# Near-equal steps with a mixed sixth transfer, and a first load issued as two partition halves, in a relu-and-row-sum kernel

## Chip, cores and metric

The kernel runs on one core of a Trainium2 chip. The metric is the device time of one execution in microseconds (us). Profiles show a slightly shorter span than that time (162.8 us for a run timed at 164.56 us), because the span counts from the first to the last recorded work. Every run quoted here was fast, with a granted clock of 1.0.

Engine names in the profile: ACT is ScalarE, DVE is VectorE, SP is SyncE. SPq and ACTq are those engines' sequencers, which issue transfers (DMAs). A transfer has "landed" when its semaphore has received the last of its increments.

## The reference

```python
x = np.random.randn(32, 512, 1024).astype(np.float32)     # 64 MiB
relu_x = np.maximum(x, 0)
out = np.sum(relu_x, axis=-1).astype(np.float32)          # (32, 512)
```

There are 16,384 rows of 1,024 floats. Each of the 128 partitions handles 128 successive rows, so the input of a partition is one contiguous stretch of 512 KiB.

## The kernel before

The rows come in seven transfers of 16 rows per partition (8 MiB, 64 KiB contiguous per partition) into three buffers, then in a tail of 8, 4, 2, 1 rows and two half-rows. All loads are issued by SyncE. In the first six transfers ("two-pass"), ScalarE applies relu in place to a step of rows and VectorE sums that step; the steps are 2, 6 and 8 rows. In the seventh transfer and in the tail ("fused"), each engine takes alternate rows and does relu and sum in one instruction. Cuts are marked with `# ...`.

```python
BIG, NBIG, NTWO, NB = 16, 7, 6, 3
STEPS, TAIL, LAST = [2, 6, 8], [8, 4, 2, 1], [512, 512]
# ...
for c in range(NBIG + 1):
    if c >= NB:
        sp.wait_ge(s_dve, len(STEPS) * (c - NB + 1))       # buffer free
    if c < NBIG:
        sp.dma_start(
            out=buf[:, c % NB, :, :], in_=xv[:, c * BIG : (c + 1) * BIG, :]
        ).then_inc(s_in[c], 16)
# ... tail loads, same form
for c in range(NTWO):
    b, r = c % NB, 0
    act.wait_ge(s_in[c], 16)
    for i, n in enumerate(STEPS):
        t = buf[:, b, r : r + n, :]
        act.activation(t, t, AF.Relu).then_inc(s_act, 1)
        dve.wait_ge(s_act, len(STEPS) * c + i + 1)
        dve.tensor_reduce(out=res[:, c * BIG + r : c * BIG + r + n],
                          in_=t, axis=X, op=ALU.add).then_inc(s_dve, 1)
        r += n
# ... seventh transfer and tail: on_dve / on_act on alternate rows
# ... the two half-rows: both on VectorE, one after the other; then the store of res
```

Of the kernel before, what the change touches and what calls it, by code (L numbers as in the profile page):

```python
# [2 lines left out]

P = 128
D = 1024
BIG = 16
NBIG = 7
NTWO = 6
NB = 3
STEPS = [2, 6, 8]  # L10
TAIL = [8, 4, 2, 1]
LAST = [512, 512]


def bass_relu_sum_kernel(
    nc: bass.Bass,
    x: bass.AP,
    out: bass.AP,
):




    fp32 = mybir.dt.float32
    ALU = mybir.AluOpType
    AF = mybir.ActivationFunctionType
    X = mybir.AxisListType.X

    B, S, _ = x.shape
    J = B * S // P  # L30
    assert BIG * NBIG + sum(TAIL) + 1 == J and sum(LAST) == D

    xv = x.rearrange("b s d -> (b s) d").rearrange("(p j) d -> p j d", p=P)
    ov = out.rearrange("b s -> (b s)").rearrange("(p j) -> p j", p=P)

    buf = nc.alloc_sbuf_tensor("buf", [P, NB, BIG, D], fp32)
    last = nc.alloc_sbuf_tensor("last", [P, LAST[1] + 1], fp32)
    res = nc.alloc_sbuf_tensor("res", [P, J], fp32)

    n_in = NBIG + len(TAIL) + 2  # L40
    s_in = [nc.alloc_semaphore(f"s_in{i}") for i in range(n_in)]
    s_act = nc.alloc_semaphore("s_act")
    s_dve = nc.alloc_semaphore("s_dve")
    s_part = nc.alloc_semaphore("s_part")
    s_tact = nc.alloc_semaphore("s_tact")
    s_tdve = nc.alloc_semaphore("s_tdve")
    s_out = nc.alloc_semaphore("s_out")

    sp, act, dve = nc.sync, nc.scalar, nc.vector


    tb = NBIG % NB
    for c in range(NBIG + 1):
        if c >= NB:
            sp.wait_ge(s_dve, len(STEPS) * (c - NB + 1))
        if c < NBIG:
            sp.dma_start(  # L57
                out=buf[:, c % NB, :, :], in_=xv[:, c * BIG : (c + 1) * BIG, :]
            ).then_inc(s_in[c], 16)
    r = 0  # L60
    tail = []
    for i, n in enumerate(TAIL):
        sp.dma_start(
            out=buf[:, tb, r : r + n, :],
            in_=xv[:, NBIG * BIG + r : NBIG * BIG + r + n, :],
        ).then_inc(s_in[NBIG + i], 16)
        tail.append((r, n, s_in[NBIG + i]))
        r += n
    sp.dma_start(
        out=buf[:, tb, r, 0 : LAST[0]], in_=xv[:, J - 1, 0 : LAST[0]]  # L70
    ).then_inc(s_in[-2], 16)
    sp.dma_start(out=last[:, 0 : LAST[1]], in_=xv[:, J - 1, LAST[0] : D]).then_inc(
        s_in[-1], 16
    )


    for c in range(NTWO):
        b, r = c % NB, 0
        act.wait_ge(s_in[c], 16)
        for i, n in enumerate(STEPS):  # L80
            t = buf[:, b, r : r + n, :]
            act.activation(t, t, AF.Relu).then_inc(s_act, 1)  # L82
            dve.wait_ge(s_act, len(STEPS) * c + i + 1)
            dve.tensor_reduce(  # L84
                out=res[:, c * BIG + r : c * BIG + r + n], in_=t, axis=X, op=ALU.add
            ).then_inc(s_dve, 1)
            r += n


    def on_act(t, acc):  # L90
        return act.activation(t, t, AF.Relu, accum_out=acc)  # L91

    def on_dve(t, acc):
        return dve.tensor_scalar(  # L94
            out=t, in0=t, scalar1=0.0, scalar2=None, op0=ALU.max, op1=ALU.add, accum_out=acc
        )

    j0 = NBIG * BIG
    for c in range(NTWO, NBIG):
        act.wait_ge(s_in[c], 16)  # L100
        dve.wait_ge(s_in[c], 16)
        for i in range(BIG):
            f = on_act if i % 2 else on_dve
            f(buf[:, c % NB, i, :], res[:, c * BIG + i : c * BIG + i + 1])
    for r, n, s in tail:
        act.wait_ge(s, 16)
        if n > 1:
            dve.wait_ge(s, 16)
        for i in range(r, r + n):
            f = on_act if n == 1 or (i - r) % 2 else on_dve  # L110
            ins = f(buf[:, tb, i, :], res[:, j0 + i : j0 + i + 1])
            if f is on_act:
                last_act = ins
    last_act.then_inc(s_tact, 1)

    dve.wait_ge(s_in[-2], 16)
    on_dve(buf[:, tb, BIG - 1, 0 : LAST[0]], last[:, LAST[1] : LAST[1] + 1]).then_inc(s_part, 1)
    dve.wait_ge(s_part, 1)
    dve.wait_ge(s_in[-1], 16)
    on_dve(last[:, :], res[:, J - 1 : J]).then_inc(s_tdve, 1)  # L120


    sp.wait_ge(s_tact, 1)
    sp.wait_ge(s_tdve, 1)
    sp.dma_start(out=ov[:, :], in_=res[:, :]).then_inc(s_out, 16)
    sp.wait_ge(s_out, 16)


# [1 line left out]
_INS = ['x']  # L130
_OUTS = [((32, 512), 'float32')]


# [21 lines left out]
```

## Time and profile before

| What | Value | Where it is read |
|---|---|---|
| time | 164.67 us median (164.54 to 165.19, 3 runs) | run times |
| load queue busy | 96.1% of 16 DMA engines' span | queue table |
| steady period of an 8 MiB transfer | 19.35 us | starts of ACT in the timeline |
| first transfer landed | 23.1 us | first relu in the timeline |
| last load landed | 158.96 us | semaphore records |
| DVE done | 161.15 us | chain of waits |

From the page of the kernel before: the busy tenths of the DMA engines and the GB/s they moved, in 40 equal slices, and the row of the load queue (packets, MB, share of the time of 16 engines).

```profile
DMA  7979979979989998998997997997998997999980
GB/s 258 515 306 467 499 322 467 515 322 451 515 370 403 515 419 354 515 419 354 515 467 306 515 499 322 467 515 338 435 515 354 419 515 338 427 419 403 411 322 16
q1 hardware_dynamic: 2016, 67.18, 96.1%
```

The transfer engines are busy from the first slice to the last. The GB/s swing because a 64 KiB packet is counted in one slice; the mean over a longer stretch says more. This is such a stretch, from 5 to 20 us; the last two columns are the DMA share and GB/s.

```profile
core 0: us, DVE busy (x) ACT busy (x) POOL busy (x), PEclk, DMA share, GB/s
5.00:20.00 15.00, 0.00 (x0) 0.00 (x0) 0.00 (x0) 1.00 1.05 450
```

The timeline of ACT (start, length, instruction, and in brackets the idle time before it and what ended it):

```profile
0.72 1.28 ACT L82 ACT_TABLE_LOAD   x1 [0.72 <-PEq L140]
23.15 14.04 ACT L82 ACTIVATE buf<-buf 128x2048 f32<-128x2048 f32 x3 [21.14 <-DMA buf<-in_x_dram]
42.45 14.04 ACT L82 ACTIVATE buf<-buf 128x2048 f32<-128x2048 f32 x3 [5.26 <-DMA buf<-in_x_dram]
61.91 14.04 ACT L82 ACTIVATE buf<-buf 128x2048 f32<-128x2048 f32 x3 [5.42 <-DMA buf<-in_x_dram]
```

ACT needs 14 us of every 19.35 us and then waits for the next load. The end of the chain of waits (start, length, what):

```profile
134.03 8.69 DVE res L84
142.72 16.28 DVE buf L94 x29
159.00 0.73 issue
159.73 0.70 DVE buf L94 x3
160.43 0.02 issue
160.46 0.69 DVE last L94 x2
```

Here, at the end only, DVE is late. The eight-row reduce of the sixth transfer ends at 142.7 us, 3.4 us after the seventh has landed, and DVE works without a pause until 161.15 us, 2.2 us behind the last load. (The row of 0.73 us "issue" is not a pause of DVE: from 142.72 to 161.15 us it was busy for 18.39 of 18.43 us.)

### The profile page before, as it was taken

How to read it: one execution, taken by the hardware profiler on the slowest of the kernel's cores; microseconds unless marked ns; L12 is line 12 of the kernel's file. 1: busy time of each engine (PE TensorE's matmuls, PEld its weight loads, DVE VectorE, ACT ScalarE, POOL GpSimd, SP SyncE). 2: the span in 40 equal slices, each digit the busy share in tenths (PEclk: the TensorE clock that was granted, in tenths of full speed). 3: DMA queues.
4: the chain of work that ended last, by engine and by line, in shares of the span. 5: the costliest groups of instructions: out<-in, count | busy, mean ns of one | idle time of the engine just before them, and what ended most of it. 6: DMA issues, size and time to landing. Idle time of an engine off the chain costs nothing.

```text
span 162.8 us, 136 instructions
## 1 busy us (share of the span) xinstructions
DVE 123.1 (76%) x52; ACT 102.7 (63%) x51; POOL 0.2 (0%) x4
## 2 busy tenths in 40 slices
DVE  0000005599988999599996999969998799999995
ACT  3000039991599807996099942999159990796880
POOL 0000000000000000000000000000000000000000
DMA  7979979979989998998997997997998997999980
GB/s 258 515 306 467 499 322 467 515 322 451 515 370 403 515 419 354 515 419 354 515 467 306 515 499 322 467 515 338 435 515 354 419 515 338 427 419 403 411 322 16
DMA packets 2016, 67.18 MB, mean 413 GB/s; under 512 B 224, under 2 KB 352, under 8 KB 736
## 3 DMA queue, kind: packets, MB, share of 16 engines
q1 hardware_dynamic: 2016, 67.18, 96.1%
HBM read 67.11 MB, written 0.07 MB: 413 GB/s over the span
## 4 chain that ended last, share of the span: by engine, by line
DMA 47%; ACT 26%; DVE 22%; another core or an unknown queue 3%; issue 1%; SPq 0%
DMA buf<-in_x_dram 47%; ACT buf L82 26%; DVE res L84 11%; DVE buf L94 10%; DVE last L94 0%; SPq L57 0%
## 5 line engine op out<-in xcount | busy, mean ns | idle before, releaser
L84 DVE TENSOR_REDUCE res<-buf 128x2 f32<-128x2048 f32 (+2 forms) x18 | 104.7, 5839 | 38.0 <-ACT buf L82 38.0
L82 ACT ACTIVATE buf<-buf 128x2048 f32<-128x2048 f32 (+2 forms) x18 | 84.2, 4743 | 47.7 <-DMA buf<-in_x_dram 47.7
L91 ACT ACTIVATE buf<-buf 128x1024 f32<-128x1024 f32 x16 | 16.7, 1045 | 7.7 <-DMA buf<-in_x_dram 7.5
L94 DVE TENSOR_SCALAR_CACHE_REDUCE buf<-buf 128x1024 f32<-128x1024 f32 (+1 forms) x16 | 17.8, 1180 | 0.0
L91 ACT ACTIVATION_READ_ACCUMULATOR buf<-buf 128x1 f32 x16 | 3.0, 187 | 0.0
L82 ACT ACT_TABLE_LOAD x1 | 1.3, 1283 | 0.7 <-PEq L140 0.7
L94 DVE DVE_READ_ACCUMULATOR buf<-buf 128x1 f32 x16 | 1.3, 82 | 0.0
L94 DVE TENSOR_SCALAR_CACHE_REDUCE last<-last 128x513 f32<-128x513 f32 x1 | 0.7, 690 | 0.0
L140 POOL MEMSET const-bfloat16-1.0<- 128x1 bf16 x1 | 0.1, 102 | 0.0
L140 POOL MEMSET const-uint8-127<- 128x1 uint8 x1 | 0.1, 101 | 0.0
L140 POOL MEMSET const-float32-0.0<- 128x1 f32 x1 | 0.1, 99 | 0.2 <-issue 0.2
L140 POOL MEMSET const-float32-1.0<- 128x1 f32 x1 | 0.1, 98 | 0.0
L94 DVE DVE_READ_ACCUMULATOR last<-last 128x1 f32 x1 | 0.1, 82 | 0.0
## 6 DMA issues: line engine op xcount, KB each, us to landing
buf<-in_x_dram SPq DMA_DIRECT2D x1, 4096.0 KB, 25.6
buf<-in_x_dram SPq DMA_DIRECT2D x1, 2048.0 KB, 30.1
buf<-in_x_dram SPq DMA_DIRECT2D x1, 1024.0 KB, 32.1
buf<-in_x_dram SPq DMA_DIRECT2D x1, 512.0 KB, 32.9
buf<-in_x_dram SPq DMA_DIRECT2D x1, 256.0 KB, 33.1
last<-in_x_dram SPq DMA_DIRECT2D x1, 256.0 KB, 33.2
buf<-in_x_dram SPq DMA_DIRECT2D x7, 35.3
out_dram<-res SPq DMA_DIRECT2D x1, 64.0 KB, 1.5
```

The costliest lines, as they stand in the source:

```text
L82: act.activation(t, t, AF.Relu).then_inc(s_act, 1)
L84: dve.tensor_reduce(out=res[:, c * BIG + r : c * BIG + r + n], in_=t, axis=X, op=ALU.add).then_inc(s_dve, 1)
L91: return act.activation(t, t, AF.Relu, accum_out=acc)
L94: return dve.tensor_scalar(out=t, in0=t, scalar1=0.0, scalar2=None, op0=ALU.max, op1=ALU.add, accum_out=acc)
L140: nc = _bacc.Bacc("TRN2", target_bir_lowering=False, num_devices=1)
```

## The change

It has two independent parts. The first takes that VectorE backlog away: the two-pass steps become 4, 5, 7; in the sixth transfer four rows are done fused (two on each engine) and the other twelve in steps of 3, 4, 5; in the tail the single row goes to VectorE and the first half-row to ScalarE. `on_dve(*row(c, i))` and `on_act(*row(c, i))` are the fused instruction on row i of transfer c. The second part is meant to start the load stream sooner: the first transfer is cut into partitions 0 to 63 (from SyncE) and 64 to 127 (from ScalarE).

```diff
-STEPS = [2, 6, 8]
+STEPS = [4, 5, 7]
+MIXED = [3, 4, 5]
@@ loads
-        if c < NBIG:
+        if c == 0:
+            for q, h in ((sp, 0), (act, P // 2)):
+                q.dma_start(
+                    out=buf[h : h + P // 2, 0, :, :], in_=xv[h : h + P // 2, 0:BIG, :]
+                ).then_inc(s_in[0] if h == 0 else s_half, 16)
+        elif c < NBIG:
             sp.dma_start(out=buf[:, c % NB, :, :], ...)          # cut
@@ two-pass transfers
+        b, steps = c % NB, STEPS if c < NTWO - 1 else MIXED
         act.wait_ge(s_in[c], 16)
+        if c == 0:
+            act.wait_ge(s_half, 16)
+        if steps is MIXED:
+            dve.wait_ge(s_in[c], 16)
+            for i in (BIG - 4, BIG - 3):
+                on_dve(*row(c, i))
         ...                                                        # relu and reduce by steps, as before
+        if steps is MIXED:
+            for i in (BIG - 2, BIG - 1):
+                on_act(*row(c, i))
@@ the first half-row
-    on_dve(buf[:, tb, BIG - 1, 0 : LAST[0]], ...).then_inc(s_part, 1)
-    dve.wait_ge(s_part, 1)
+    act.wait_ge(s_in[-2], 16)
+    on_act(buf[:, tb, BIG - 1, 0 : LAST[0]], ...).then_inc(s_tact, 1)
+    dve.wait_ge(s_tact, 1)
```

More of the change, by code (lines that the diff above doesn't have):

```diff
@@ L43, in bass_relu_sum_kernel @@
     s_dve = nc.alloc_semaphore("s_dve")
-    s_part = nc.alloc_semaphore("s_part")
     s_tact = nc.alloc_semaphore("s_tact")
     s_tdve = nc.alloc_semaphore("s_tdve")
+    s_half = nc.alloc_semaphore("s_half")
     s_out = nc.alloc_semaphore("s_out")
@@ L54, in bass_relu_sum_kernel @@
         if c >= NB:
-            sp.wait_ge(s_dve, len(STEPS) * (c - NB + 1))
-        if c < NBIG:
+            sp.wait_ge(s_dve, 3 * (c - NB + 1))
+        if c == 0:
[4 more added lines that the diff above has]
+        elif c < NBIG:
             sp.dma_start(
@@ L74, in bass_relu_sum_kernel @@
     )
-    for c in range(NTWO):
-        b, r = c % NB, 0
-        act.wait_ge(s_in[c], 16)
-        for i, n in enumerate(STEPS):
-            t = buf[:, b, r : r + n, :]
-            act.activation(t, t, AF.Relu).then_inc(s_act, 1)
-            dve.wait_ge(s_act, len(STEPS) * c + i + 1)
-            dve.tensor_reduce(
-                out=res[:, c * BIG + r : c * BIG + r + n], in_=t, axis=X, op=ALU.add
-            ).then_inc(s_dve, 1)
-            r += n
     def on_act(t, acc):
@@ L96, in on_dve, with row @@
         )
+    def row(c, i):
+        return buf[:, c % NB, i, :], res[:, c * BIG + i : c * BIG + i + 1]
+    for c in range(NTWO):
+        b, steps = c % NB, STEPS if c < NTWO - 1 else MIXED
+        act.wait_ge(s_in[c], 16)
+        if c == 0:
[4 more added lines that the diff above has]
+                on_dve(*row(c, i))
+        r = 0
+        for i, n in enumerate(steps):
+            t = buf[:, b, r : r + n, :]
+            act.activation(t, t, AF.Relu).then_inc(s_act, 1)
+            dve.wait_ge(s_act, 3 * c + i + 1)
+            dve.tensor_reduce(
+                out=res[:, c * BIG + r : c * BIG + r + n], in_=t, axis=X, op=ALU.add
+            ).then_inc(s_dve, 1)
+            r += n
+        if steps is MIXED:
+            for i in (BIG - 2, BIG - 1):
+                on_act(*row(c, i))
     j0 = NBIG * BIG
@@ L102, in bass_relu_sum_kernel @@
         for i in range(BIG):
-            f = on_act if i % 2 else on_dve
-            f(buf[:, c % NB, i, :], res[:, c * BIG + i : c * BIG + i + 1])
+            (on_act if i % 2 else on_dve)(*row(c, i))
     for r, n, s in tail:
-        act.wait_ge(s, 16)
         if n > 1:
-            dve.wait_ge(s, 16)
+            act.wait_ge(s, 16)
+        dve.wait_ge(s, 16)
         for i in range(r, r + n):
-            f = on_act if n == 1 or (i - r) % 2 else on_dve
-            ins = f(buf[:, tb, i, :], res[:, j0 + i : j0 + i + 1])
-            if f is on_act:
-                last_act = ins
-    last_act.then_inc(s_tact, 1)
-    dve.wait_ge(s_in[-2], 16)
-    on_dve(buf[:, tb, BIG - 1, 0 : LAST[0]], last[:, LAST[1] : LAST[1] + 1]).then_inc(s_part, 1)
-    dve.wait_ge(s_part, 1)
+            f = on_act if (i - r) % 2 else on_dve
+            f(buf[:, tb, i, :], res[:, j0 + i : j0 + i + 1])
+    act.wait_ge(s_in[-2], 16)
+    on_act(buf[:, tb, BIG - 1, 0 : LAST[0]], last[:, LAST[1] : LAST[1] + 1]).then_inc(s_tact, 1)
+    dve.wait_ge(s_tact, 1)
     dve.wait_ge(s_in[-1], 16)
     on_dve(last[:, :], res[:, J - 1 : J]).then_inc(s_tdve, 1)
-    sp.wait_ge(s_tact, 1)
     sp.wait_ge(s_tdve, 1)
```

## The prediction

The prediction numbers its transfers in two ways: "transfer 5" and "transfer 6" count from 0 and are the sixth and the seventh of this text, while its "sixth transfer" is the sixth here too.

> **What bounds the kernel now.** The load. The page's queue table gives the load queue 96.1% of 16 engines' span; the slices show it moving at about 430 GB/s from end to end. In the timeline ScalarE (ACT) starts on transfers 1 to 6 at 42.45, 61.91, 81.28, 100.61, 119.96 and 139.32 us: one 8 MiB transfer per 19.35 us, 433 GB/s. The list of transfers shows 64 KiB packets of 2.42 us, back to back on every engine. The first transfer lands at 23.1 us, because the first packets start only between 1.74 and 2.71 us and take 3.1 us. The last load lands at about 158.95 us. VectorE (DVE) ends at 161.15 us and the store takes 1.5 us more, so compute adds about 2.2 us behind the last load. In the chain of waits DVE is behind: it starts transfer 6 at 142.64 us, though that landed at 139.3, because the six-row and eight-row reduces of transfer 5 last until then.
>
> **Steps 4,5,7 and mixed sixth transfer.** From the groups by form, a reduce costs 0.143 + 1.068 us per row, a relu 0.21 + 0.85 us per row. Per transfer ACT stays at 14.05 us; DVE ends 21.7 us after landing instead of 22.75, still behind the load's 19.35, so nothing moves before the end. The sixth transfer (two fused rows on each engine at 1.14 and 1.04 us, then 3+4+5) ends 18.0 us after landing: DVE meets transfer 6 on time, 3.3 us earlier than now. In the tail both engines keep up. The last half-row (0.69 us) then starts on its data, or just after ACT's half-row, at 0.1 us behind the landing: DVE ends about 0.8 us after the last landing instead of 2.2. Worth 1.4 us.
>
> **The split first transfer.** Meant gain: two issuers halve the 0.97 us ramp of first packets, up to 0.5 us earlier for every later landing. [...] All 16 engines would take a SyncE packet, then a ScalarE packet, nearly in step[...]. Estimate: the packets of the first transfer take 3.5 to 4.7 us instead of 2.42; with 8 per engine, the first transfer lands 9 to 18 us later, and since the load queue never idles afterwards, all of it reaches the end. [...]
>
> **Sum.** 164.67 - 1.4 + about 14 = 177 us. [...] The range must span both: 162.7 to 183. Faster by over 2%: 0.02; within 2%: 0.28; slower by over 2%: 0.70.
>
> **What would show it.** Right: ACT's first relu starts at 32 to 41 us instead of 23.15; first-transfer packets well over 2.42 us; low GB/s in the first slices; then again 19.35 us per transfer; DVE starts transfer 6 at its landing; DVE ends 0.7 to 0.9 us after the last load. Wrong: first landing near 22.7 us with 2.42 us packets; or a later landing but with the loss caught up afterwards.
>
> **What would make it wrong.** [...] writes of both queues overlapping in one engine; or ScalarE issuing so late that the halves overlap differently.

Passages that rest on what no trace or run of this case shows are cut, here and in the expectations below; the cuts are marked. The sum came to 177 us and is printed whole, 164.67 - 1.4 + about 14. A second sum, for a split that loses nothing: 162.8 to 163.3 us, which is 164.67 - 1.4 less up to 0.5 us of meant gain. The two sums are the "both" of the range. The packets of 3.5 to 4.7 us are the author's estimate, 1.4 to 1.9 times the 2.42 us of the trace before; that trace has no half transfer, so the factor was not shown. Eight such packets per engine give the 9 to 18 us.

## The result and the profile after

The changed kernel took 182.92 us (median of 4 runs, 182.38 to 183.05), the kernel before 164.61 us (4 runs). The ratio is 1.1097, with a 95% interval of 1.1064 to 1.1131: clearly slower. Ratios here are the mean time of one kernel's fast runs over that of the other's in the same rounds, so they are not quite the ratios of the quoted medians.

From the page after, the same lines:

```profile
DMA  9999998879999899999988999999889999799993
GB/s 232 232 232 232 232 217 174 174 174 421 464 464 391 377 391 464 464 464 464 449 377 348 450 464 464 464 464 420 377 362 464 464 464 464 341 420 406 428 392 116
q1 hardware_dynamic: 1952, 62.98, 86.5%
q10 hardware_dynamic: 80, 4.19, 10.8%
```

The transfer engines are still busy all the time, but in the first nine slices they move about half as much (174 to 232 GB/s, against 341 to 464 in all later ones but the last). Busy is not the same as moving data at full rate. The second queue, q10, is ScalarE's half of the first transfer. Between 5 and 20 us:

```profile
5.00:20.00 15.00, 0.00 (x0) 0.00 (x0) 0.00 (x0) 1.00 0.97 210
```

That is 210 GB/s in place of 450. Both figures are rough, because a packet counts whole where it starts (210 is exactly 48 packets of 64 KiB in 15 us). By the time of a packet, below, full rate is 16 x 64 KiB in 2.42 us, or 433 GB/s, and the first transfer of the changed kernel ran at 16 x 64 KiB in 4.87 us, or 215 GB/s. The timeline of ACT after:

```profile
0.73 0.56 ACTq L61 DMA_DIRECT2D buf<-in_x_dram  x1
42.98 1.28 ACT L108 ACT_TABLE_LOAD   x1 [42.98 <-DMA buf<-in_x_dram]
44.28 14.04 ACT L108 ACTIVATE buf<-buf 128x4096 f32<-128x4096 f32 x3
61.94 14.04 ACT L108 ACTIVATE buf<-buf 128x4096 f32<-128x4096 f32 x3 [3.62 <-DMA buf<-in_x_dram]
81.28 14.04 ACT L108 ACTIVATE buf<-buf 128x4096 f32<-128x4096 f32 x3 [5.31 <-DMA buf<-in_x_dram]
```

The first transfer has landed at 42.9 us instead of 23.1. From then on the period is 19.35 us as before (61.94 to 81.28), so the loss is not won back: the last load landed 19.4 us later than before. The end of the chain of waits:

```profile
143.50 34.22 DMA buf<-in_x_dram
177.72 0.02 issue
177.75 0.73 ACT buf L86 x2
178.48 0.02 issue
178.50 0.70 DVE last L89 x2
```

This part went as intended: the chain is the load up to 177.72 us and then only ACT's half-row and DVE's half-row. The last load landed at 178.32 us by its semaphore, and DVE was done at 179.20, 0.9 us later instead of 2.2.

The transfer records of the trace show the loss packet by packet. All 64 KiB packets of the first transfer, sixteen in each group (as many as the page counts DMA engines), in order of start:

```
                     before                    after
group   queue  median us of a packet   queue  median us of a packet
1       q1     3.12                    q1     4.84
2       q1     2.42                    q10    4.87
3       q1     2.42                    q1     4.87
4       q1     2.42                    q10    4.87
5       q1     2.45                    q1     4.86
6       q1     2.42                    q10    4.87
7       q1     2.42                    q1     4.86
8       q1     2.42                    q10    4.87
next transfer  2.42                           2.98, then 2.42
```

Sixteen packets of SyncE's half and sixteen of ScalarE's half take turns, and each packet takes twice as long, 4.87 us against 2.42. By these medians the eight groups add up to 18.8 us more, and the first packet of the next transfer to 0.6 us more: 19.4 us together. The sixteen packets of a group, all of one half of the partitions, start within 0.7 to 1.5 us.

### The profile page after: what moved, and what is told of

Same layout as the page of the kernel before. It is cut to its first block, busy times and chain, and to the rows that moved or that the text cites. A ratio compares the mean times of both kernels' runs of the same rounds, so it can differ in the third digit from the quotient of the medians.

```text
span 180.8 us, 145 instructions
## 1 busy us (share of the span) xinstructions
DVE 121.8 (67%) x56; ACT 101.0 (56%) x55; POOL 0.2 (0%) x4
## 4 chain that ended last, share of the span: by engine, by line
DMA 62%; ACT 24%; DVE 9%; another core or an unknown queue 2%; SPq 1%; issue 0%; ACTq 0%
DMA buf<-in_x_dram 62%; ACT buf L108 23%; DVE res L110 8%; SPq L71 1%; ACT L108 1%; ACT buf L86 0%; DVE last L89 0%; ACTq L100 0%
## 5 line engine op out<-in xcount | busy, mean ns | idle before, releaser
L110 DVE TENSOR_REDUCE res<-buf 128x4 f32<-128x4096 f32 (+3 forms) x18 | 100.3, 5603 | 54.5 <-ACT buf L108 54.5
L108 ACT ACTIVATE buf<-buf 128x4096 f32<-128x4096 f32 (+3 forms) x18 | 80.8, 4553 | 24.9 <-DMA buf<-in_x_dram 24.9
L86 ACT ACTIVATE buf<-buf 128x1024 f32<-128x1024 f32 (+1 forms) x18 | 18.4, 1022 | 9.7 <-DMA buf<-in_x_dram 9.7
L89 DVE TENSOR_SCALAR_CACHE_REDUCE buf<-buf 128x1024 f32<-128x1024 f32 x18 | 21.0, 1216 | 2.7 <-DMA buf<-in_x_dram 2.5
```

The lines of the kernel that those rows point to most:

```text
L86: return act.activation(t, t, AF.Relu, accum_out=acc)
L89: return dve.tensor_scalar(out=t, in0=t, scalar1=0.0, scalar2=None, op0=ALU.max, op1=ALU.add, accum_out=acc)
```

## Theories and experiments

**Destination theory.** The time of a packet depends on which partitions its transfer writes: a half of neighbouring partitions, 0 to 63 or 64 to 127, is slow whoever issues it. The profile after fits this (4.87 us a packet in place of 2.42) but does not prove it. Packet times for pieces that had not run yet are estimates: about one, two or four times the 2.42 us of a 64 KiB packet of the whole transfer. **Rivals:** two queues that take turns cost the time; the number of partitions, or the reads from memory, cost it; it belongs to the cold start; or the new steps hold up the load.

Experiments change the changed kernel unless it is said otherwise. Their edits are shown shortened: unchanged lines, and the semaphore counts that go with more or fewer pieces, are left out. The experiments ran in four jobs, on more than one chip, so the small differences between jobs are not interpreted. Each job also ran the kernel before: 164.4 us in the first, 164.4 to 164.6 us in the others.

### 1. The steps without the split

```diff
-            for q, h in ((sp, 0), (act, P // 2)):
-                q.dma_start(...)                                   # two halves
+            sp.dma_start(out=buf[:, 0, :, :], in_=xv[:, 0:BIG, :]).then_inc(s_in[0], 16)
```

> The changed kernel with the first transfer whole again, from SyncE. [...] (the split alone costs 19.4 us[...]; the steps win about 1.4 us): 163.2 us, range 162.9 to 163.6, first relu at about 23.2 us, last load at about 158.9 us, DVE done 0.8 us after it. Rival theory (the new steps or the late ACT table load hold the load up): well over 164.6 us.

Measured: 162.87 us (6 runs, 162.64 to 163.88), ratio 0.9912 (0.9893 to 0.9931), a hair below the expected range. The steps are a gain of 1.5 us, and the split alone spoiled it. The end of its chain of waits:

```profile
124.00 34.14 DMA buf<-in_x_dram
158.13 0.02 issue
158.16 0.73 ACT buf L83 x2
158.89 0.02 issue
158.91 0.70 DVE last L86 x2
```

The last load landed at 158.75 us (158.96 in the kernel before), and DVE was done at 159.61 instead of 161.15. So 1.3 us of the 1.5 us of DVE's earlier end are its backlog. How the gain divides among the new steps, the mixed sixth transfer and the new order in the tail was not tested.

### 2. Two issuers, but halves of rows instead of partitions

```diff
-            for q, h in ((sp, 0), (act, P // 2)):
-                    out=buf[h : h + P // 2, 0, :, :], in_=xv[h : h + P // 2, 0:BIG, :]
+            for q, h in ((sp, 0), (act, BIG // 2)):
+                    out=buf[:, 0, h : h + BIG // 2, :], in_=xv[:, h : h + BIG // 2, :]
```

> The changed kernel with the first transfer split by rows instead of partitions: rows 0 to 7 of all 128 partitions from SyncE, rows 8 to 15 from ScalarE. Still two issuers and two queues that alternate in each engine. [...] 32 KiB packets of 1.21 us, no loss, first transfer landed by 23.5 us, 163.2 us within 0.5. Rival theory (two queues that alternate in one engine cost the time): packets of about 2.43 us, first landing near 43 us, about 183 us.

Measured: 162.91 us (4 runs), ratio 0.9905. The packets of the two queues take turns just as in the changed kernel, and from the second group on take 1.21 us for 32 KiB, which is the rate of 2.42 us for 64 KiB. The same stretch from 5 to 20 us:

```profile
5.00:20.00 15.00, 0.00 (x0) 0.00 (x0) 0.00 (x0) 1.00 1.00 433
```

Alternating queues cost nothing (experiments 9 and 11 show it with 64 KiB packets of 2.42 us too). Two issuers also win nothing: the time is that of experiment 1.

### 3. Both partition halves from one issuer

```diff
-            for q, h in ((sp, 0), (act, P // 2)):
+            for q, h in ((sp, 0), (sp, P // 2)):
```

> The changed kernel with both partition halves issued by SyncE, one after the other, on one queue. [...] packets of 4.86 us, about 183 us, first relu near 43 us. Two-queue theory: the loss is gone, about 163 us.

Measured: 184.02 us (4 runs), ratio 1.1188. There is only one queue, and the loss stays; median packets took 4.92 to 5.12 us. With experiment 2 this rules the two queues out. Why the packets were a little slower than 4.86 us stays open. The other run with both halves on one queue, experiment 8, shows the same median of 5.12 us, and the two runs with the halves on two queues 4.87 us (the changed kernel) and 4.96 us (experiment 4).

### 4. The kernel before with only the split

```diff
@@ against the kernel before
-        if c < NBIG:
+        if c == 0:                                                 # two halves, as in the change
+            ...
+        elif c < NBIG:
```

> The kernel before with only the split of its first transfer. [...] the whole of the last DVE backlog stays, so 164.6 plus 19.4, 184.0 us within 0.7; the rest of the change is then worth 1.1 to 1.4 us. If the loss needs the new steps, it stays near 164.6 us.

Measured: 184.46 us (4 runs), ratio 1.1212. In this job the split costs 184.46 - 164.40 = 20.1 us with the old steps. The new steps have no part in the loss. Experiments 1 and 4 also show that the two parts of the change add up: -1.5 and +20.1 make +18.5, against +18.3 measured for both together.

### 5. The same input, another destination

```diff
-            for q, h in ((sp, 0), (act, P // 2)):
-                    out=buf[h : h + P // 2, 0, :, :], in_=xv[h : h + P // 2, 0:BIG, :]
+            for q, d, h, n in ((sp, 32, 0, 64), (act, 96, 64, 32), (act, 0, 96, 32)):
+                    out=buf[d : d + n, 0, :, :], in_=xv[h : h + n, 0:BIG, :]
```

> Wrong result on purpose. SyncE's 64-partition transfer reads the same half of the input as in the changed kernel but writes partitions 32 to 95; ScalarE's half is sent to 96 to 127 and 0 to 31 as two 32-partition transfers. [...] SyncE's packets take 2.42 us and ScalarE's 4.86 us; 4 of each per engine, so half the loss: first relu near 33.3 us, about 173.2 us. Rival theory (64 partitions, or this pattern of reads from memory, is slow whatever the destination): SyncE's packets stay at 4.86 us, about 183 us.

Measured: 174.61 us (2 runs), ratio 1.0622; wrong results. SyncE's transfer reads the same half of the input as in the changed kernel and has 64 partitions as there; only its destination moved from 0 to 63 to 32 to 95. The packets of the first transfer, by the trace:

```
group            1      2      3      4      5      6      7      8
issuer        ScalarE ScalarE SyncE  SyncE ScalarE SyncE ScalarE SyncE
median us       4.88   5.12   2.97   2.42   4.85   3.41   4.77   3.32
```

SyncE's packets went from 4.87 us to between 2.4 and 3.4 us, ScalarE's stayed near 4.9. So neither the count of partitions nor the reads of that half are what is slow: the destination is. The 3.3 us packets overlap in time with the tails of slow ones; that this is why they missed 2.42 us, and why the time missed 173.2 by 1.4 us, is a guess. SyncE's four groups add up to 12.1 us where 9.7 was expected, which is more than the whole miss.

### 6 and 7. Quarters and eighths of neighbouring partitions

```diff
-            for q, h in ((sp, 0), (act, P // 2)):
-                    out=buf[h : h + P // 2, 0, :, :], in_=xv[h : h + P // 2, 0:BIG, :]
+            for h in range(0, P, 32):                              # 16 in the other run
+                q = sp if h < P // 2 else act
+                    out=buf[h : h + 32, 0, :, :], in_=xv[h : h + 32, 0:BIG, :]
```

> First transfer in four 32-partition quarters, two from each issuer. [...] packets of 4.86 us and about 183 us, the same as the changed kernel. Rival theory (the rate falls with the number of partitions): packets of 9.7 us, about 221 us.

> First transfer in eight 16-partition pieces, four from each issuer. [...] packets of 9.7 us, first landing near 81 us, about 221 us. Rival (rate falls with the number of partitions): packets of 19.4 us, about 299 us. Rival (loss is that of two queues or of the split as such): about 183 us.

Measured: 182.53 us for quarters (2 runs, ratio 1.1104), 217.25 us for eighths (2 runs, ratio 1.3216). From 5 to 20 us for the quarters, and from 5 to 70 us for the eighths:

```profile
5.00:20.00 15.00, 0.00 (x0) 0.00 (x0) 0.00 (x0) 1.00 0.99 210
```

```profile
5.00:70.00 65.00, 0.00 (x0) 0.00 (x0) 0.00 (x0) 1.00 1.00 113
```

Half as many partitions at a time changed next to nothing (median packets of 4.93 us against 4.87), a quarter as many nearly halved the rate (9.30 us). Why 64 and 32 neighbours are alike and 16 are not is not shown. The eighths came 4 us under the expected 221 us because their packets took 9.3 us and not 9.7.

### 8. The fourth transfer split instead of the first

```diff
-        if c == 0:
-            for q, h in ((sp, 0), (act, P // 2)):
+        if c == 3:
+            for q, h in ((sp, 0), (sp, P // 2)):
```

> First transfer whole; the fourth is split into partition halves, both from SyncE. [...] the loss belongs to the transfer, not to the start: packets of 4.86 us for that transfer only, then about 183 us, first relu at 23.2 us and 38.7 us between the third landing and the fourth. Rival (the loss belongs to the cold start): about 163 us.

Measured: 184.76 us (2 runs), ratio 1.1240. In the timeline of ACT the fourth transfer is the one that is late:

```profile
62.34 14.04 ACT L109 ACTIVATE buf<-buf 128x4096 f32<-128x4096 f32 x3 [5.96 <-DMA buf<-in_x_dram]
103.03 7.97 ACT L109 ACTIVATE buf<-buf 128x4096 f32<-128x4096 f32 x2 [26.65 <-DMA buf<-in_x_dram]
```

It starts 40.7 us after the third instead of 19.35 (38.7 was expected; the packets took 5.12 us and not 4.86, as in experiment 3). The loss followed the split from the first transfer to the fourth; it is not a matter of the cold start, and with three buffers the load did not make it up.

### 9. Even and odd partitions

```diff
-            for q, h in ((sp, 0), (act, P // 2)):
-                    out=buf[h : h + P // 2, 0, :, :], in_=xv[h : h + P // 2, 0:BIG, :]
+            for q, h in ((sp, 0), (act, 1)):
+                    out=buf[h:P:2, 0, :, :], in_=xv[h:P:2, 0:BIG, :]
```

> First transfer split into even partitions (SyncE) and odd partitions (ScalarE). [...] in the form '[...] at the same moment': packets of 4.86 us, about 183 us. In the form '[...] the transfer reaches': packets of 2.42 us, about 163 us.

Measured: 163.13 us (2 runs), ratio 0.9916, packets of 2.42 us from the second group on:

```profile
5.00:20.00 15.00, 0.00 (x0) 0.00 (x0) 0.00 (x0) 1.00 1.05 454
```

Two transfers of 64 partitions from two issuers lose nothing when each takes every second partition: 2.42 us a packet, against 4.87 us for 64 neighbours. The two forecasts above are those of two forms of the theory. They differed in an assumption about which engine carries which partitions; the trace does not number the engines, so that was not shown, and this run does not decide between the forms. Experiment 11 has two forecasts for the same reason.

### 10 and 11. Every eighth and every fourth partition

```diff
-            for q, h in ((sp, 0), (act, P // 2)):
-                    out=buf[h : h + P // 2, 0, :, :], in_=xv[h : h + P // 2, 0:BIG, :]
+            for h in range(8):                                     # 4 in the other run
+                q = sp if h < 4 else act
+                    out=buf[h:P:8, 0, :, :], in_=xv[h:P:8, 0:BIG, :]
```

> First transfer in eight 16-partition pieces as in the eighths, but piece h takes every eighth partition (h, h+8, ... h+120)[...] packets of 4.86 us, about 183 us, against 217 us for 16 neighbouring partitions. Rival theory (partitions spread over the whole range are fast, as even and odd were): packets of 2.42 us, about 163 us.

> First transfer in four 32-partition pieces, piece h takes every fourth partition (h, h+4, ... h+124)[...], while the quarters of 32 neighbouring partitions [...] took 182.5 us. [...] packets of 2.42 us, about 163 us. [...] packets of 4.86 us, about 183 us.

Measured: every eighth partition 183.60 us (2 runs, ratio 1.1153), every fourth 163.22 us (2 runs, ratio 0.9916). The stretch from 5 to 20 us, every eighth and then every fourth:

```profile
5.00:20.00 15.00, 0.00 (x0) 0.00 (x0) 0.00 (x0) 1.00 0.98 210
```

```profile
5.00:20.00 15.00, 0.00 (x0) 0.00 (x0) 0.00 (x0) 1.00 1.04 450
```

Every eighth partition is spread over the whole range, and yet at half rate, 4.88 us a packet; every fourth is at full rate, 2.42 us. So spreading as such does not help. Neither does the number of partitions tell the rate: 64 took 4.87 us as neighbours and 2.42 as every second, 32 took 4.93 and 2.42 (every fourth), 16 took 9.30 and 4.88 (every eighth). Nor are neighbours always at half rate: 32 to 95 took 2.42 to 3.41 us (experiment 5). What it is in the choice of partitions that sets the rate is not shown. All shapes in one table (a window's GB/s counts whole packets, so the time of a packet, the median of the second to the eighth group, is the better measure):

```
first transfer in pieces of        GB/s of the window   packet us   time us
128 partitions (exp. 1)                  437              2.42        162.9
every 2nd, 64 partitions (exp. 9)        454              2.42        163.1
every 4th, 32 partitions (exp. 11)       450              2.42        163.2
every 8th, 16 partitions (exp. 10)       210              4.88        183.6
64 neighbours from 0 or 64 (change)      210              4.87        182.9
32 neighbours (exp. 6)                   210              4.93        182.5
16 neighbours (exp. 7)                   113              9.30        217.3
```

## Why the prediction was right or wrong

- **What bounds the kernel: right.** The load is the only thing that counts until the last landing. A loss in the first transfer came through to the end: the first landing moved by 19.8 us, the last by 178.32 - 158.96 = 19.4 us.
- **The steps, 1.4 us: right.** Alone they gave 1.5 us (experiment 1). The timeline and the chain show the mechanism: in the changed kernel DVE started on the seventh transfer at its landing (158.70 us) and ended 0.9 us behind the last load.
- **The loss by the split: right in direction, too small in size.** The mis-sized step is "the packets of the first transfer take 3.5 to 4.7 us", summed up as "about 14". That packet time was the author's estimate; the trace before has no half transfer, so nothing in it gave the factor. The packets took 4.87 us, twice 2.42, and the split cost 19.8 us in the changed kernel's first landing (9 to 18 were predicted), 19.4 us in its last, and 20.1 us of time in experiment 4. The first relu started at 44.28 us, not at 32 to 41. With 19.4 for 14, the sum would have been 164.67 - 1.4 + 19.4 = 182.7 us. That the range of 162.7 to 183 still held the measured 182.92 is in part luck: its own largest loss, 18 us, gives 164.67 - 1.4 + 18 = 181.3 us, and only the slack above that reached the measured time.
- **The meant gain, "two issuers halve the 0.97 us ramp of first packets, up to 0.5 us": not seen.** First packets started from 2.05 to 2.74 us, against 1.74 to 2.71 before. The ramp was shorter only because its beginning was later; the last engine started no sooner. (These are single profiles: in that of experiment 1, with the whole transfer, first packets started from 1.74 to 3.33 us.) Issuing a 64-partition half took 0.54 us on SyncE and 0.56 us on ScalarE, against 0.38 us for the whole transfer. Experiment 2, without the loss (1.21 us for 32 KiB), won nothing over experiment 1 either (162.91 and 162.87 us).
- **Not foreseen:** ScalarE's table load moved from 0.72 us to 42.98 us, behind the wait for the first half. That ScalarE now issues a transfer is not needed for that: in experiment 3 it issues none, and the table load still comes at 44.52 us. In every run with a second wait before the first relu it comes late (from 23.38 us in experiment 2 to 77.66 us in experiment 7), and with one wait (the kernel before, experiments 1 and 8) it comes at 0.72 us. It delays the first relu by 1.3 us. In experiment 2 it sits there too, at 23.38 us, and the time is the same, so it costs nothing here.
- **Left open:** what in the choice of partitions makes a packet take 2.42, 4.9 or 9.3 us, and which engine carries which partitions; the trace shows neither.

The best version seen is experiment 1, the change without its split: 162.87 us, 0.9% faster than the kernel before: clear of the noise.

## What to carry to other kernels

Before a transfer is cut, measure the time of a packet for the very partitions that each piece writes; the number of issuers, queues or partitions did not tell it here. A half made of neighbouring partitions ran at half the rate (4.87 us for 64 KiB), while halves made of rows (1.21 us for 32 KiB), or of even and odd partitions (2.42 us for 64 KiB), ran at full rate. Transfer engines that show as fully busy may still move half the data (a DMA share of 0.97 at 210 GB/s here, 1.05 at 450 before), so look at GB/s and at the time of one packet beside the busy share. In this load-bound kernel such a loss reached the end whole, in the first transfer (20.1 us of time in experiment 4) as in the fourth (184.76 us in experiment 8). Judge the parts of a change one by one, because a good 1.5 us was hidden here under a bad 20 us.
